# Delta rule: three buffers for a head's chain, the state load inside the chunk stage, and gate columns made in front as pairs

## The chip, the cores and the metric

The kernel runs on one core of a Trainium2 chip. The core has TensorE (PE in the profile, with its weight loads as PEld), VectorE (DVE), ScalarE (ACT), GpSimd (POOL) and SyncE (SP). Each engine takes its instructions in order. Here SP issues nearly all transfers between the main memory and the core's memory. The metric is device microseconds for one execution. Before the change three runs took 2188.87, 2191.32 and 2192.17 us: a median of 2191.32.

## What is computed

One layer of an encoder, for 512 prompt tokens and 8 x 16 sample tokens, 640 rows together, all in fp32:

```python
z = x @ w_in                                   # 2048 -> 12312 columns
q_a, k_a, v_a, f_a, gate_a, qkv_b, a_b, beta_b, gate_b, m_a, m_b = jnp.split(z, SPLIT_IDX, axis=-1)
# branch A: attention with forget gates, 8 heads of 128
y_a = (o_a * jax.nn.silu(gate_a)) @ w_out_fox
# branch B: delta rule, 8 heads of 128 x 128
conv = jax.nn.silu(sum(xpad[:, i:i + n_tok] * gdn_conv_w[i] for i in range(CONV_W)))
q_b, k_b, v_b = jnp.split(conv, [GDN_KEY_WIDTH, 2 * GDN_KEY_WIDTH], axis=-1)
o_b, s_new = gated_delta_chunked(q_b, k_b, v_b, g, beta, s0)
o_b = rms_norm(o_b, gdn_norm_w)
y_b = (o_b * jax.nn.silu(gate_b)) @ w_out_gdn
h = (jax.nn.sigmoid(m_a) * y_a + jax.nn.sigmoid(m_b) * y_b) @ w_out
x1 = layer_norm(DEEPNORM_ALPHA * x + h, ln_g, ln_b)
x_out = x1 + jax.nn.sigmoid(x1 @ w_pl_gate) * e    # e: rms_norm(p @ w_pl_proj)
```

`gated_delta_chunked` takes each chunk of tokens, solves a unit lower triangular system built from keys, decays and betas, and carries a 128 x 128 state from chunk to chunk. The sample rows start from stored states `s0`.

## The kernel before

**Columns.** The projections are made in columns of 128 output channels by 640 rows. A product in fp32 is made of three products of halves (high times high, high times low, low times high) in a fast fp32 form. In `column` (with `mm6`, L380 and L381) each of the 16 slices of the inner dimension needs 6 matmuls of 128x320. In `pair` (L458) two columns are made together, by a scheme with 7 products of half size instead of 8: 7 forms of 8 slices of 3 matmuls. A pair needs sums of weights, which VectorE makes (`w_sum`, L316) or, for some later columns, GpSimd in advance (`weight_sums`, loads L288, sums L292, stores L298). Weights come in tiles of 128x1024 (`wr`, L266), and are split into high and low by ScalarE (`wh`, L326) and VectorE (`wl`, L327), up to five pieces of 512 ahead of TensorE.

**Stages.** `front` makes the first columns, the values, and then `PAIRS` = 19 pairs: four of the attention gate, two of values, eleven of the merge gates (`FRONT` = 22 columns), two of query and key for heads 3 and 6. `phase_fox` makes the remaining queries and keys, and runs the attention between them. `phase_gdn` makes, per head of the delta rule, a column each of q, v, k and gate (`gq`, `gv`, `gk`, `gg`), and after some heads a merge column (`FILL`, `mcol`). Then come four plain and four half pairs of columns of `w_out_fox`, and `tail`.

**What sets the order.** There is one program order per engine, written by the Python code as it runs. While a column is made, `tick` is called once per slice (in a pair, once per two slices, so always once per six large matmuls). Generators in several lanes stand beside it; a tick lets each lane go a step, if its last `yield n` is n ticks ago and a planner's clock says that its inputs are there. The planner knows matmuls and the three other engines, but not when transfers land. `until(cond)` lets ticks pass without a column.

**A head of the delta stage.** `conv_silu` makes q, k, v. `gdn` makes decays, norms, and `lt` and `qk` (L948). `gdn_blocks` stores the 32x32 diagonal blocks (`ld`, L967), loads them spread over 80 partitions (`lanes`, L970), solves them on GpSimd in 31 steps (L978, L980), stores the result (`xd`, L985) and loads it as `u0` (L988), then the state `st` of the sample rows (L992). After `yield 8` it hands over to `gdn_chunks`, which copies `u0` on GpSimd (L1007) and runs `gdn_pro` (transposes `u0` on VectorE, L1101, first product L1110, then the four chunks) beside `gdn_dec` (sample rows, first use of `st` at L1059). `gdn_out` norms the output, multiplies it with the gate loaded from memory and stores it. The buffers of a head (`kt`, `vr`, `lt`, `qk`, `gr`, `kq`) exist twice, so `gdn` waits until the chunks of head h-2 are done (`chdone`), and `gdn_blocks` until those of h-1 are.

The gate column of a head goes through `silu_evac` (L807 to L809) and to memory in the delta stage.

Of the kernel before, what the change touches and what calls it, by code (L numbers as in the profile page):

```python
# [52 lines left out]
class Kernel:  # L53
# [8 lines left out]
    FRONT = 32 - 3 - 7  # L62
    PAIR0, PAIRS = 6, 6 + FRONT // 2 + 2
    BETWEEN = 6,
    APART = 3, 6
    FILL = 1, 1, 1, 0, 0, 0, 0, 4
# [430 lines left out]
    def consts2(self):  # L497
# [5 lines left out]
        self.nw = self.cv[:, 96:97]  # L503
# [297 lines left out]
    def silu_evac(self, ps, dst, tag):  # L801

        nc = self.nc
        for hf in range(2):
            sl = slice(hf * HALF, (hf + 1) * HALF)
            th = self.zt([P, HALF], tag, 1, "sc")
            nc.scalar.activation(th, ps[hf], AF.Tanh, scale=0.5)  # L807
            nc.vector.tensor_single_scalar(dst[:, sl], ps[hf], 0.5, op=ALU.mult)
            nc.vector.scalar_tensor_tensor(out=dst[:, sl], in0=th, scalar=1.0, in1=dst[:, sl], op0=ALU.add, op1=ALU.mult)  # L809


    def scale_e(self, re):

        nc = self.nc
        tags, e = [("kt", 2), ("vr", 2), ("lt", 2), ("qk", 2)], {}
# [30 lines left out]
    def conv_silu(self, strip, ct, h, c, dst):  # L846
# [18 lines left out]
        while self.done[c] < h - 2 + c % 2:  # L865
            yield
# [10 lines left out]
    def gdn(self, h, kq, v):  # L877
        nc, cb = self.nc, self.cb
        while not self.scaled or self.chdone < h - 2 or min(self.ready) < h:
            yield  # L880
        gr = self.zt([P, T], "gr", 2)
# [3 lines left out]
        kt = self.zt([P, 5, P], "kt", 2)  # L885
        vr = self.zt([P, 5, P], "vr", 2)
# [40 lines left out]
        cs = self.zt([P, 5, 5], "cs", 3)  # L927
# [12 lines left out]

        lt = self.zt([P, 5, P], "lt", 2)
        qk = self.zt([P, 5, P], "qk", 2)
# [19 lines left out]
    def gdn_blocks(self, h, kq, lt, qk, qg, kt, vr, cs):  # L962
# [24 lines left out]
        u0 = self.zt([P, 5, 32], "u0")  # L987
        nc.sync.dma_start(out=u0, in_=bass.AP(self.xd.tensor, self.xd.offset, [[32, P], [4096, 5], [1, 32]]))  # L988
        while self.chdone < h - 1:
            yield 2  # L990
        st = self.zt([P, 8, P], "st")
        nc.sync.dma_start(out=st, in_=self.i["st"][h])  # L992
        yield 8
        self.bdone = h
        self.chunks["gens"].append(self.gdn_chunks(h, kq, lt, qk, qg, kt, vr, cs, u0, st))

    def gdn_chunks(self, h, kq, lt, qk, qg, kt, vr, cs, u0, st):

        nc, uu = self.nc, self.uu
# [51 lines left out]
    def gdn_dec(self, h, qk, kt, vr, cs, st):  # L1051
# [3 lines left out]
        yield 6  # L1055
# [41 lines left out]
    def gdn_pro(self, h, kq, lt, qk, qg, kt, vr, cs, u0):  # L1097
# [4 lines left out]
        t1 = self.t1  # L1102
# [31 lines left out]
        x2 = self.zt([P, 4, 64], "sx2", 1, "x2")  # L1134
        nc.scalar.copy(out=x2[64:128].rearrange("p a b -> p (a b)"), in_=px[64:128, 0:256])
        yield 2
        px = self.sps()
        for t in range(4):
            nc.tensor.matmul(px[0:64, t * 64:(t + 1) * 64], x2[64:128, t, :], uu[64:128, t, 64:128],
                             start=True, stop=True)  # L1140
# [43 lines left out]
    def run(self, ctx):  # L1184
# [16 lines left out]
        self.sgd = [dr([P, T], F32, name=f"sgd{i}") for i in range(H)]  # L1201
        self.sgf = [dr([P, T], F32, name=f"sgf{i}") for i in range(H)]
# [43 lines left out]
    def front(self, work):  # L1246
# [122 lines left out]
        def vals(x, hf, z, u=None):  # L1369
# [7 lines left out]
            def close(h=2 * (n - 4) + 4 + x):  # L1377
# [28 lines left out]
        def heads(x, hf, z, u=None):  # L1406
# [8 lines left out]

            def close(h=self.APART[n - 6 - self.FRONT // 2]):
                if x == 0:
                    nc.scalar.mul(o, o, FOX_SCALE)
                nc.sync.dma_start(out=self.qkd[h, x], in_=m[x])
                if x:  # L1420
                    nc.sync.dma_start(out=self.o["fk"][h], in_=m[x])
# [4 lines left out]
        def weights():  # L1426
# [3 lines left out]
            yield from self.weight_sums([t[:, x:x + 256] for t in ws for x in (0, 256)], slice(0, 10), (6, 4, 2))  # L1430
        self.sums["gens"].append(weights())
        for n in range(self.PAIRS):
# [21 lines left out]
            self.pair(xf, gates if n < 4 else vals if n < 6 else merges if n < 6 + self.FRONT // 2 else heads, back)  # L1454
            if n < 4:
                self.ng += 2
            elif 6 <= n < 6 + self.FRONT // 2:
                self.nm += 2
# [4 lines left out]
    def phase_fox(self, work):  # L1463
# [14 lines left out]
        self.sums["gens"].append(self.weight_sums([ws[:, x:x + 256] for x in range(0, 1024, 256)], slice(10, 12),  # L1478
# [56 lines left out]
    def phase_gdn(self, conv, work):  # L1535
# [6 lines left out]
        self.sums["gens"].append(self.weight_sums([ws[:, x:x + 171] for x in range(0, 684, 171)], slice(12, None),  # L1542
                                                  (8, 6, 4)))
        self.uu = self.zt([P, 5, P], "uu")
        self.t1 = self.zt([64, 4, 64], "t1")
        self.kpad = self.zt([P, 8, 32], "kpad")
        self.gpad = self.zt([P, 8, 32], "gpad")
        for x in (self.uu, self.t1, self.kpad, self.gpad):
            nc.gpsimd.memset(x, 0.0)

        self.kqs = [self.zt([P, 2, T], f"kq{i}") for i in range(2)]
# [3 lines left out]
        self.scaled, self.chdone, self.bdone = False, -1, -1  # L1555
        self.ends["gens"].append(self.scale_e(re))
        self.untapped = 0
        for h in range(H):
            for c in range(4):
                acc = self.column()[0]  # L1560
                kq = self.kqs[h % 2]
                if c == 1:
                    v = self.zt([P, T], "v")
                if c == 3:
                    sg = self.zt([P, T], "sg")
                    self.silu_evac(acc, sg, "gth")
                    nc.sync.dma_start(out=self.sgd[h], in_=sg)
                else:
                    self.until(lambda: self.untapped == 0)
                    ct = 8 * (0, 2, 1)[c] + h  # L1570
                    self.untapped += 1
                    stp = self.strip_evac(acc, ct)
                    conv["gens"].append(self.conv_silu(stp, ct, h, c,
                                                       v if c == 1 else kq[:, 1 - c // 2, :]))
# [10 lines left out]
        def load(k, tag, to=raw):  # L1585
            to[k] = self.zt([P, {"ws": 684, "lanes": 1024}.get(tag, T)], tag, 2 if tag in ("kt", "vr", "lt", "qk", "gr") else 1,
# [742 lines left out]
def _layout(a):  # L2329
# [18 lines left out]
    for b in [*bg, *_wblock(seg["v"])[4:], *m[:nf], *[x[h] for h in Kernel.APART for x in (bq, bk)]]:  # L2348
# [10 lines left out]
    for h in range(H):  # L2359
        bl += [gq[h], gv[h], gk[h], gg[h]]  # L2360
# [80 lines left out]
```

## Time and profile before

| | |
|---|---|
| median of three runs | 2191.32 us |
| the profiled execution | 2187.32 us, of it 2185.5 us span |
| TensorE busy | 2165.9 us (99%) |
| VectorE, ScalarE, GpSimd busy | 67%, 43%, 26% |
| mean granted TensorE clock | 0.999 |
| front with its pairs | up to about 573 us |
| delta stage, from its first GpSimd work | from about 878 us |
| last use of a solved head, L1110 | 1586 us |

Matmuls overlap in the engine: a row's mean duration is that of one matmul from start to end, and is longer than the distance to the next. Counts in a stretch are those of the records; a plain fp32 product leaves two records. A row of waits says who ended an engine's idle time, not who caused the lateness.

### The profile page before, as it was taken

The page shows a single profiled execution, that of the slowest core. Times are in us where ns is not written, and L with a number is a line of the kernel's source. Part 1 is how long each engine was busy: PE and PEld are TensorE (multiplying, and loading weights), DVE is VectorE, ACT ScalarE, POOL GpSimd, SP SyncE. Part 2 cuts the span into 40 slices and gives each one's busy share as a digit, 9 for nine tenths or more (in the row PEclk, how much of TensorE's full clock was granted, in tenths as well). Part 3 has the DMA queues.
Part 4 walks back from the last instruction along what each step waited for, and adds up shares of the span by engine and source line. Part 5 has one row for each costly group of instructions (what it writes and reads, how often), then busy time and mean ns, then how long its engine had stood idle before and what let it go on. Part 6 is the DMA issues. An engine that isn't in the chain of part 4 may idle for free. (4 is left out here: it accounts for less than half of the span.)

```text
span 2185.5 us, 41824 instructions
## 1 busy us (share of the span) xinstructions
PE 2165.9 (99%) x15582; PEld 2099.0 (96%) x15582; DVE 1458.6 (67%) x2705; ACT 931.3 (43%) x2065; POOL 578.1 (26%) x1046
## 2 busy tenths in 40 slices
PE   9999999999999999999999999999999999999998
PEld 7799999999999999999999999999999999999998
DVE  5877677667545546755556566565657787789987
ACT  4344444444333335344345345345443343354544
POOL 0023223333011110216817637556600000011100
PEclk9999999999999999999999999999999999999999
DMA  6356665666687876854454444446566656674465
GB/s 233 104 184 197 198 189 185 196 193 204 236 317 256 309 267 199 290 167 126 121 156 131 130 126 142 123 131 196 167 243 245 221 167 205 195 274 133 149 229 171
DMA packets 222284, 421.12 MB, mean 193 GB/s; under 512 B 33768, under 2 KB 118840, under 8 KB 222080
## 3 DMA queue, kind: packets, MB, share of 16 engines
q1 hardware_dynamic: 222080, 418.45, 58.7%
q8 instruction: 122, 2.00, 0.4%
q14 instruction: 82, 0.67, 0.1%
HBM read 323.29 MB, written 95.07 MB: 191 GB/s over the span
## 5 line engine op out<-in xcount | busy, mean ns | idle before, releaser
L327 DVE TENSOR_TENSOR wl<-wr,wh 128x512 fp32r<-128x512 f32 x636 | 450.2, 717 | 349.0 <-ACT wh L326 340.1
L326 ACT CAST wh<-wr 128x512 fp32r<-128x512 f32 x636 | 388.5, 618 | 316.8 <-PE g L381 136.2
L380 PE MATMUL g<-xh,wh 128*128 128x320 f32 (+1 forms) x1152 | 375.9, 326 | 0.0
L380 PE MATMUL g<-xl,wh 128*128 128x320 f32 (+1 forms) x1152 | 356.1, 309 | 0.6 <-DVE xl L355 0.6
L381 PE MATMUL g<-xh,wh 128*128 128x320 f32 x1152 | 356.3, 309 | 0.0
L381 PE MATMUL g<-xl,wh 128*128 128x320 f32 x1152 | 355.9, 309 | 0.0
L380 PE MATMUL g<-xh,wl 128*128 128x320 f32 (+1 forms) x1152 | 355.8, 309 | 0.0
L381 PE MATMUL g<-xh,wl 128*128 128x320 f32 x1152 | 355.6, 309 | 0.0
L458 PE MATMUL g<-xh,wh 128*128 128x320 f32 (+1 forms) x1104 | 343.9, 311 | 2.7 <-ACT m L1240 1.6
L458 PE MATMUL g<-xl,wh 128*128 128x320 f32 (+1 forms) x1104 | 341.9, 310 | 0.6 <-DVE xl L355 0.6
L458 PE MATMUL g<-xh,wl 128*128 128x320 f32 (+1 forms) x1104 | 342.0, 310 | 0.0
L292 POOL TENSOR_TENSOR ws<-ws 128x171 f32<-128x171 f32 (+2 forms) x184 | 137.7, 748 | 658.0 <-DMA ws<-in_w 650.1
L380 PEld LDWEIGHTS g<-xh,wh 128*128 128x128 f32 x1152 | 217.0, 188 | 12.4 <-issue 8.6
L458 PE MATMUL g<-t,wh 128*128 128x320 f32 (+1 forms) x992 | 220.2, 310 | 0.0
L381 PEld LDWEIGHTS g<-xh,wh 128*128 128x128 f32 x1152 | 217.2, 189 | 1.0
L380 PEld LDWEIGHTS g<-xl,wh 128*128 128x128 f32 x1152 | 216.9, 188 | 1.1 <-DVE xl L355 1.1
L381 PEld LDWEIGHTS g<-xl,wh 128*128 128x128 f32 x1152 | 216.6, 188 | 0.0
L380 PEld LDWEIGHTS g<-xh,wl 128*128 128x128 f32 x1152 | 216.4, 188 | 0.2
L381 PEld LDWEIGHTS g<-xh,wl 128*128 128x128 f32 x1152 | 216.4, 188 | 0.0
L458 PEld LDWEIGHTS g<-xh,wh 128*128 128x128 f32 x1104 | 207.9, 188 | 4.5 <-ACT m L1240 2.1
L458 PEld LDWEIGHTS g<-xl,wh 128*128 128x128 f32 x1104 | 207.6, 188 | 1.1 <-DVE xl L355 1.1
L458 PEld LDWEIGHTS g<-xh,wl 128*128 128x128 f32 x1104 | 208.0, 188 | 0.0
(443 smaller groups left out, 3774.1 us busy)
## 6 DMA issues: line engine op xcount, KB each, us to landing
wr<-in_w SPq DMA_DIRECT2D x258, 512.0 KB
kc<-in_kc SPq DMA_DIRECT2D x32, 512.0 KB
vc<-in_vc SPq DMA_DIRECT2D x32, 512.0 KB
ws<-in_w SPq DMA_DIRECT2D x96, 128.0 KB
md<-m SPq DMA_DIRECT2D x32, 320.0 KB
t<-md SPq DMA_DIRECT2D x32, 320.0 KB
sr<-in_w SPq DMA_DIRECT2D x19, 512.0 KB
ws<-in_w SPq DMA_DIRECT2D x100, 85.5 KB
```

The costliest lines, as they stand in the source:

```text
L292: nc.gpsimd.tensor_tensor(out=o, in0=x, in1=y, op=op)
L326: nc.scalar.copy(out=hi, in_=src)
L327: nc.vector.tensor_tensor(out=lo, in0=src, in1=hi.bitcast(F32), op=ALU.subtract)
L380: nc.tensor.matmul(ps[0], whl[w], xhl[o][:, a], start=(first and x == 0), stop=(last and x == 2))
L381: nc.tensor.matmul(ps[1], whl[w], xhl[o][:, b], start=(first and x == 0), stop=(last and x == 2))
L458: nc.tensor.matmul(ps, a[:, w], b, start=(k == 0 and n == 0 and not more), stop=(k == last and n == 2), skip_group_check=True)
```

## The change

Eight more columns, the delta rule's gates, are made in the front as four pairs (`NG` = 8 gate columns and 8 more, stored in `sgf`, of which `sgd` is now the second half). One pair of merge columns leaves the front (`FRONT` = 20) and its two columns join the delta stage as fillers after heads 3 and 4. `PAIRS` becomes 22. A factor 0.5 of the gate moves into the norm weight `nw`. The GpSimd weight sums are dealt out as 12, 2 and 3 to the three stages; it was 10, 2 and 5.

In the delta stage `kt`, `vr`, `qk`, `gr` and the keys get three buffers. `lt` keeps two and is guarded by a new mark, `merged`, set once the chunk stage has read it. `gdn` may start when the chunks of head h-3 are done, and `gdn_blocks` loads `u0` (two buffers now) when those of h-2 are. The state is loaded by `gdn_chunks` itself. `x2` shares the tile of `t1`. Last, the scratch for software-made transfers is 1024 bytes.

```diff
-    FRONT = 32 - 3 - 7
-    PAIR0, PAIRS = 6, 6 + FRONT // 2 + 2
+    FRONT = 32 - 5 - 7
+    NG = 8
+    PAIR0, PAIRS = 6, NG + 2 + FRONT // 2 + 2
-    FILL = 1, 1, 1, 0, 0, 0, 0, 4
+    FILL = 1, 1, 1, 1, 1, 0, 0, 4
...
-        while self.done[c] < h - 2 + c % 2:
+        while self.done[c] < h - (2, 1, 3)[c]:
             yield
...
-        while not self.scaled or self.chdone < h - 2 or min(self.ready) < h:
+        while not self.scaled or self.chdone < h - 3 or min(self.ready) < h:
             yield
-        gr = self.zt([P, T], "gr", 2)
+        gr = self.zt([P, T], "gr", 3)
...
+        while self.merged < h - 2:
+            yield
         lt = self.zt([P, 5, P], "lt", 2)
-        qk = self.zt([P, 5, P], "qk", 2)
+        qk = self.zt([P, 5, P], "qk", 3)
...
         nc.sync.dma_start(out=self.xd, in_=x.rearrange("p c i -> p (c i)"))
         yield 5
-        u0 = self.zt([P, 5, 32], "u0")
+        while self.chdone < h - 2:
+            yield 2
+        u0 = self.zt([P, 5, 32], "u0", 2)
         nc.sync.dma_start(out=u0, in_=bass.AP(self.xd.tensor, self.xd.offset, [[32, P], [4096, 5], [1, 32]]))
-        while self.chdone < h - 1:
-            yield 2
+        yield 4
+        self.chunks["gens"].append(self.gdn_chunks(h, kq, lt, qk, qg, kt, vr, cs, u0))
+
+    def gdn_chunks(self, h, kq, lt, qk, qg, kt, vr, cs, u0):
+
+        nc, uu = self.nc, self.uu
         st = self.zt([P, 8, P], "st")
         nc.sync.dma_start(out=st, in_=self.i["st"][h])
-        yield 8
-        self.bdone = h
-        self.chunks["gens"].append(self.gdn_chunks(h, kq, lt, qk, qg, kt, vr, cs, u0, st))
...
         self.ob = ob = self.zt([P, 5, P], "ob")
-        yield 6
+        yield 9
...
-            yield from self.weight_sums([t[:, x:x + 256] for t in ws for x in (0, 256)], slice(0, 10), (6, 4, 2))
+            yield from self.weight_sums([t[:, x:x + 256] for t in ws for x in (0, 256)], slice(0, 12), (6, 4, 2))
...
-            for c in range(4):
+            for c in range(3):
                 acc = self.column()[0]
-                kq = self.kqs[h % 2]
+                kq = kqs[:, h % 3:4 + h % 2:3 + h % 2 - h % 3]
                 if c == 1:
                     v = self.zt([P, T], "v")
-                if c == 3:
-                    sg = self.zt([P, T], "sg")
-                    self.silu_evac(acc, sg, "gth")
-                    nc.sync.dma_start(out=self.sgd[h], in_=sg)
...
-    nc = _bacc.Bacc("TRN2", target_bir_lowering=False, num_devices=1)
+    nc = _bacc.Bacc("TRN2", target_bir_lowering=False, num_devices=1, dynamic_dma_scratch_size=1024)
```

The diff shows little of how instructions move. Two places on SP do. The first is the last head's chain, head 7. Before (`out_stp` is the end of head 6's chunks, `xd` the solve's store of head 7, `og` a gate load, `fd` and `wr` belong to the columns):

```order
L1180 DMA out_stp<-S 128x128
L1017 DMA og<-sgd_174 128x640
L985 DMA xd<-sx 80x256
L266 DMA wr<-ws102b 128x1024
L1680 DMA fd_18360<-fx 128x640
L988 DMA u_19082<-xd 128x5x32
L992 DMA st<-in_st 128x1024
L1680 DMA fd_18361<-fx 128x640
```

The same place in the changed program:

```order
L978 DMA xd<-sx 80x256
L267 DMA wr<-in_w 128x1024
L1667 DMA fd_18356<-fx 128x640
L983 DMA u_18890<-xd 128x5x32
L1172 DMA out_stp<-S 128x128
L991 DMA st<-in_st 128x1024
L267 DMA wr<-ws102S_191 128x1024
L1009 DMA og<-sgf_182 128x640
```

The end of head 6's chunks now stands behind the solve's store and the `u0` load of head 7, and the state load follows it: before, head 6 was over when head 7's solve ended.

The second place is the border from `front` to `phase_fox`. Before (`xq` reloads parts of x, `qkd` and `out_fk` store the last pair, then `q` and `k` are the attention's first loads):

```order
L1449 DMA xq<-in_xT 128x320 x8
L266 DMA wr<-in_w 128x1024
L1419 DMA qkd_189<-m_1163 128x640
L1421 DMA out_fk<-m_1163 128x640
L1419 DMA qkd_188<-m_1162 128x640
L1492 DMA q<-qkd_184 128x640
L1492 DMA k<-qkd_185 128x640
```

In the changed program:

```order
L1441 DMA xq<-in_xT 128x320 x8
L267 DMA wr<-in_w 128x1024
L1411 DMA qkd_189<-m_1165 128x640
L1413 DMA out_fk<-m_1165 128x640
L1411 DMA qkd_188<-m_1164 128x640
L299 DMA ws128S_227<-ws 128x256
L299 DMA ws128b<-ws 128x256
L299 DMA ws128S_228<-sb 128x256
L299 DMA ws128S_230<-sb 128x256
L1485 DMA q<-qkd_184 128x640
L1485 DMA k<-qkd_185 128x640
```

Four stores of the last GpSimd weight sum now stand between the last pair's stores and the attention's first loads.

74 lines of the change are left out of this document (32 added, 42 removed).

## The prediction

> **What bounds the kernel now.** I read the page first, then busy time by stretch, then the waits of TensorE, then the timeline of the delta stage. The page:
>
> ```profile
> span 2185.5 us, 41824 instructions
> PE 2165.9 (99%) x15582; PEld 2099.0 (96%) x15582; DVE 1458.6 (67%) x2705; ACT 931.3 (43%) x2065; POOL 578.1 (26%) x1046
> PEclk9999999999999999999999999999999999999999
> ```
>
> TensorE is busy from end to end at full granted clock; no other engine passes 67%. Time can only come from fewer or cheaper matmuls, or from its few gaps. The next view is busy time in stretches of 100 us: one stretch in the front's pairs, two in the delta stage, and the end.
>
> ```profile
> core 0: us, PE busy (x) PEld busy (x) DVE busy (x) ACT busy (x) POOL busy (x), PEclk, DMA share, GB/s
> 300.00:400.00 100.00, 100.00 (x683) 100.00 (x682) 70.98 (x94) 40.40 (x76) 31.13 (x30) 1.00 0.59 187
> 1200.00:1300.00 100.00, 98.64 (x798) 93.45 (x797) 57.38 (x134) 42.62 (x121) 52.99 (x121) 1.00 0.43 130
> 1400.00:1500.00 100.00, 98.94 (x750) 95.85 (x749) 57.30 (x137) 48.78 (x153) 68.09 (x137) 1.00 0.41 130
> 2100.00:2186.00 86.00, 78.03 (x526) 77.76 (x524) 68.82 (x121) 36.96 (x60) 0.00 (x0) 0.97 0.56 187
> ```
>
> In the front nothing but large matmuls runs: 683 in 100 us, so one large matmul costs **0.1464 us**, while the page's durations of about 309 ns overlap. In the delta stage TensorE idles about 1 us in 100; only the last 86 us have a real hole (8 us), and nothing there changes. Who makes TensorE wait:
>
> ```profile
> engine line waited for: us in total, times, longest us
> PE s L1110 <- DVE m L1101: 2.7, 3, 1.4
> ```
>
> The longest entry, 2.7 us, is the first product of a head's chunk waiting for the transpose of its solved blocks. The change works at exactly that place.
>
> **The matmuls.** A plain column is 16 slices of 6 matmuls, 96; a pair of columns is 7 forms of 8 slices of 3, 168 instead of 192. Before there are 6 + 22/2 + 2 = 19 front pairs, after 8 + 2 + 20/2 + 2 = 22. Eight gate columns leave the delta stage and two merge columns join it (FILL sums to 9, it was 7): six plain columns fewer. So +3 x 168 - 6 x 96 = **-72 matmuls**, and 72 x 0.1464 = **-10.5 us**. The front grows by 3 x 168 x 0.1464 = 73.8 us, the delta stage loses 84.3 us.
>
> The row gives 146.4 ns for 320 columns. The Trainium skill, "TensorE: Matmul & The Clock Gate", section "Back-to-back issue gap", gives N/2.4 + 2.5 ns for isolated matmuls, 135.8 ns for N = 320, and says that the weight loads set the spacing too; by that formula the saving would be 9.8 us, an estimate. The trace has the larger spacing, and PEld is as busy as PE beside it.
>
> **Work that moves without a price.** The gate's evacuation leaves the delta stage and a tanh and a multiply of 640 columns per gate join the front:
>
> ```profile
> L809 DVE SCALAR_TENSOR_TENSOR sg<-sc,sg 128x320 f32<-128x320 f32 x16 | 9.3, 581 | 0.5
> L808 DVE TENSOR_SCALAR sg<-g 128x320 f32<-128x320 f32 x16 | 7.8, 490 | 12.4 <-ACT sc L807 12.4
> L1362 DVE SCALAR_TENSOR_TENSOR m<-sa,m 128x640 f32<-128x640 f32 x8 | 6.6, 821 | 3.5 <-ACT sa L1361 3.5
> L316 DVE TENSOR_TENSOR sr<-wr,sr 128x1024 f32<-128x1024 f32 x38 | 50.0, 1316 | 0.0
> L292 POOL TENSOR_TENSOR ws<-ws 128x171 f32<-128x171 f32 x100 | 65.5, 655 | 71.5 <-DMA ws<-in_w 66.5
> L292 POOL TENSOR_TENSOR ws<-ws 128x169 f32<-128x169 f32 x20 | 12.5, 626 | 17.6 <-DMA ws<-in_w 16.5
> ```
>
> 17.1 us of VectorE leaves the delta stage and 6.6 us joins the front; each new pair also needs its weight sums, two of 1.3 us and two much like them. VectorE has 29 us idle in each 100 there while TensorE is full, so this costs nothing as long as casts stay ahead; without that cover the three pairs' sums, some 16 us, would show. GpSimd makes five weight sums in the delta stage (65.5 + 12.5 us, 15.6 each); three remain, and 31 us leave it. The fox stage keeps two, and the front, where GpSimd is 31% busy, makes two more. The halved norm weight is one tiny extra operation. The smaller scratch only frees memory: all but 204 of 222284 DMA packets are on the hardware queue, and their issuing rows are SP's.
>
> **Front to fox.** At the front's end SP now has the last weight sum's stores ahead of the fox stage's first loads, and the first ScalarE casts of that stage stand in line behind those loads. Times before, at that border:
>
> ```profile
> 573.46 0.31 PE L380 MATMUL g<-xh,wh 128*128 128x320 f32 x1
> 575.97 0.32 SPq L1419 DMA_DIRECT2D qkd<-m  x1
> 578.25 0.32 SPq L1492 DMA_DIRECT2D q<-qkd  x1
> 575.85 0.60 ACT L326 CAST wh<-wr 128x512 fp32r<-128x512 f32 x1
> 581.62 0.51 ACT L657 CAST qh<-q 128x384 fp32r<-128x384 f32 x1 [5.16 <-DMA q<-qkd]
> 584.46 1.29 DVE L327 TENSOR_TENSOR wl<-wr,wh 128x512 fp32r<-128x512 f32 x2
> ```
>
> The load of q waits 2.3 us for the last store to land. ScalarE stands 5.16 us; the next weight piece is ready at 584.46 + 1.29/2, about 585.1. Five pieces of 24 matmuls (3.5 us each) are ahead, so TensorE needs the sixth at 573.46 + 17.6 = 591.1: 6 us to spare. Four more stores at the row's 0.32 us each add 1.3 us, and if the last lands as late as this one, q is 1 to 4 us later: inside the 6. Price 0; if 4 became 10, it would be 4 us.
>
> **The head's chain.** Per head: the blocks go to memory (L967), GpSimd solves them, the result is stored (L985), u0 is loaded (L988), transposed (L1101), and TensorE's L1110 uses it. Heads 1, 4, 5, 7 and the one row of head 6:
>
> ```profile
> 1100.80 0.43 SPq L988 DMA_DIRECT2D u<-xd  x1
> 1108.13 0.44 PE L1110 MATMUL s<-m,lt 32*32 32x32 f32 x16
> 1354.11 0.38 SPq L988 DMA_DIRECT2D u<-xd  x1
> 1366.93 0.44 PE L1110 MATMUL s<-m,lt 32*32 32x32 f32 x16
> 1374.99 1.77 SPq L967 DMA_DIRECT2D ld<-lt  x4
> 1435.43 0.34 SPq L985 DMA_DIRECT2D xd<-sx  x1
> 1437.09 0.38 SPq L988 DMA_DIRECT2D u<-xd  x1
> 1443.34 0.44 PE L1110 MATMUL s<-m,lt 32*32 32x32 f32 x16 [1.06 <-DVE m L1101]
> 1458.52 1.98 SPq L967 DMA_DIRECT2D ld<-lt  x4
> 1528.31 1.77 SPq L967 DMA_DIRECT2D ld<-lt  x4
> 1580.03 0.33 SPq L985 DMA_DIRECT2D xd<-sx  x1
> 1581.75 0.37 SPq L988 DMA_DIRECT2D u<-xd  x1
> 1585.84 0.31 DVE L1101 STREAM_TRANSPOSE m<-u 128x128 f32<-128x128 f32 x1 [2.25 <-DMA u<-xd]
> 1586.20 0.44 PE L1110 MATMUL s<-m,lt 32*32 32x32 f32 x16
> ```
>
> From load to use the last head took 4.45 us, the shortest and with the transpose already waiting; heads 1, 4, 5 took 7.3, 12.8, 6.25, so they have 2.9, 8.4 and 1.8 us in hand. The program now spaces the start by 4 ticks after the u0 load instead of 8. A tick is six large matmuls, 0.88 us, so 3.5 us go. That alone would give 0.6, 0, 1.7 and 3.5 us of wait, for eight heads twice that, 11.6 us.
>
> The other way to see it is by the period. Last head: store of blocks to solve's end 51.7 us (1528.31 to 1580.03), to first use 57.9 us. Head 5, with weight sums in GpSimd's queue, took 60.4 us to the solve's end. What TensorE has to do meanwhile: from 1458.52 to 1528.31 are 69.8 us with four columns, 4 x 96 x 0.1464 = 56.2, which leaves 13.6 us of the chain's own products. With three columns it is 42.2 + 13.6 = 55.8 us. Heads 0 to 4 still get a fourth column (a merge); heads 5 to 7 have three, and stand **2.1 us** short of 57.9 even with no weight sum near. The blocks go one head at a time, and 51.7 + 1.7 to the u0 load fits into 55.8, so the lack does not pile up. Three heads at 2.1 are 6.3 us, less the 2.7 already waited: **+3.6 us**. Lower end: -2.7, all present waits gone, since 31 us of weight sums leave this queue and a third buffer lets a head's products begin earlier. Upper end: each of the three like head 5, 60.4 + 6.2 (1580.03 to 1586.20) = 66.6, or 10.8 short, 32.4 - 2.7 = +29.7. I take +3.6, nearest the last head's row, because the sums should be over by then:
>
> ```profile
> 883.23 2.32 POOL L292 TENSOR_TENSOR ws<-ws 128x171 f32<-128x171 f32 x4 [3.54 <-DMA ws<-in_w]
> 1522.57 1.11 POOL L292 TENSOR_TENSOR ws<-ws 128x169 f32<-128x169 f32 x2
> 1582.17 0.73 SPq L992 DMA_DIRECT2D st<-in_st  x1
> 1588.53 0.64 PE L1059 MATMUL s<-st,kpad 128*32 128x128 f32 x16
> ```
>
> Five sums take 640 us, 128 each, so three end some 384 us into the stage. Head 5's blocks leave 1375.0 - 883.2 = 492 us in now, and 56 us earlier after the change (six gate columns fewer, two merge columns more): 436. The state, loaded just behind u0 now and at the chunk's start after the change, costs nothing: its first use (L1059) stands nine ticks, 7.9 us, behind the load, and the last head used it 6.4 us after issue without waiting.
>
> Sum: -10.5 + 3.6 = **-6.9 us**. The profiled execution took 2187.3 us (span 2185.5 and 1.8 around it): 2180.4. The median shown lies 4 us above it, so I write 2191.3 - 6.9 = **2184 us**.
>
> **Rivals.**
> 1. *All of it arrives*, and the chain's waits vanish in the third buffer: 10.5 to 13.2 us, 2179 us. For it: the waits now are 2.7 us in eight heads. Against: 55.8 below 57.9. Chance 0.25.
> 2. *The waits eat the gain*: heads 5 to 7, and one or two more, wait 3 to 4 us each, some 11 us: 2190 us. For it: heads 1, 5 and 7 have at most 2.9 us in hand and lose 3.5. Chance 0.18.
> 3. *Slower: GpSimd's solve sets the pace.* Place: L1110 of heads 5 to 7 (and with it SP, which stands at the solve's store with weight loads behind it). Price 10.8 us a head, net +19.2: 2210 us. It beats the saving once a head needs (10.5 + 2.7)/3 = 4.4 us more than 55.8, so from 60.2 us on. For it: head 5's 60.4 us to the solve's end alone. Against: fewer weight sums there. Chance 0.11.
> 4. *The border front to fox* starves TensorE because q comes over 6 us later: about 4 us lost, 2188 us. Chance 0.06.
>
> On rival 3: by the Trainium skill, "TensorE: Matmul & The Clock Gate", Part 1, a pause of about 3.4 us lets the clock fall to half until a further 3.4 us of work; by that each such wait would cost 1.7 us more, an estimate. The rows show 1.00 through the stage and 0.97 only in the last stretch, where TensorE does pause.
>
> **How the numbers follow.** The forecast has 0.40. What a measurement of this kernel can tell from no change is about 0.2%, 4.4 us. Faster: rival 1 whole (0.25), the forecast but for its upper tail (0.34), parts of 2 and 4 (0.06): 0.65. Slower: rival 3 and a tail of 2: 0.13. The rest 0.22. The range 2175 to 2196 holds the forecast (2180 to 2188 by itself), rivals 1, 2 and 4, and leaves out rival 3 and runs below the lower end.
>
> **What would show it.** Large matmuls 72 fewer at 0.146 us; the front's end near 573.5 + 73.8 = 647 us; PE 99%; a line of waits at the first product of the chunk (L1102 after the change) between 3 and 10 us; no ScalarE wait over 11 us for q. Wrong if that line exceeds 15 us, or if PE idles at the border, or if the front's pairs run slower than 683 in 100 us with three more of them.

## The result, and the profile after

The changed kernel takes 2214.38 us (median of four runs, 2210.96 to 2218.18) beside 2191.15 us for the kernel before on the same chip: a ratio of 1.0108, 95% interval 1.0085 to 1.0131. It is 23 us slower, where 2184 us were forecast. The profiled executions are 2187.32 and 2211.32 us, 24.0 apart. First the page of the changed kernel:

```profile
span 2209.5 us, 41696 instructions
PE 2166.9 (98%) x15510; PEld 2097.0 (95%) x15510; DVE 1489.1 (67%) x2726; ACT 944.3 (43%) x2086; POOL 572.6 (26%) x1031
PEclk9999999999999999999999999999999999999999
```

The 72 matmuls are gone (15582 to 15510 records). Yet TensorE is busy 1.0 us *longer*, and its idle time, span less busy time, went from 19.6 to 42.6 us. By the forecast's own count it should be busy 2165.9 - 10.5 = 2155.4 us. So the 24 us are -10.5 for the matmuls, +23.0 of idle time, and +11.5 of matmuls that ran slower (+1.0 measured, -10.5 expected). Busy time by stretch says where; first after, then one row of before (columns: stretch, its length, TensorE's busy time and records, granted clock, DMA share, GB/s):

```profile
0.00:640.00 640.00, 635.67 (x4189) 1.00 0.59 190
640.00:700.00 60.00, 54.80 (x418) 0.97 0.85 288
700.00:1000.00 300.00, 299.86 (x2465) 1.00 0.80 269
1000.00:1660.00 660.00, 636.53 (x4797) 0.99 0.45 140
```

```profile
1000.00:1660.00 660.00, 655.26 (x4989) 1.00 0.48 151
```

5.2 us are lost between 640 and 700 us, where the front goes over to the softmax stage, and 23.5 us in the delta stage, where 4.7 were lost before. The waits of TensorE in the changed kernel (in total, times, longest):

```profile
PE s L1102 <- DVE m L1093: 9.9, 2, 6.4
PE s L880 <- DVE kqs L858: 7.2, 3, 5.1
PE s L748 <- ACT qh L659: 3.8, 1, 3.8
PE s L1079 <- POOL vm L1063: 1.8, 1, 1.8
```

L1102 is the first product of a head's chunk, which was L1110; L880 are the transposes of a head's q, k and v; L748 the first scores of the softmax stage. The last head, from the timelines of all engines (the first line is the store of its blocks):

```profile
1522.12 1.91 SPq L960 DMA_DIRECT2D ld<-lt  x4
...
1527.52 3.96 SPq L1575 DMA_DIRECT2D ogr<-ogd  x5
1531.53 0.77 SPq L963 DMA_DIRECT2D lanes<-ld  x1
1538.48 0.93 POOL L971 TENSOR_TENSOR sx<-eye,lanes 80x248 f32<-80x248 f32 x1 [14.60 <-DMA lanes<-ld]
1578.68 0.33 SPq L978 DMA_DIRECT2D xd<-sx  x1
1580.80 0.37 SPq L983 DMA_DIRECT2D u<-xd  x1
1585.09 0.31 DVE L1093 STREAM_TRANSPOSE m<-u 128x128 f32<-128x128 f32 x1 [9.34 <-DMA u<-xd]
1585.45 0.64 PE L1102 MATMUL s<-m,lt 32*32 32x32 f32 x16 [6.41 <-DVE m L1093]
```

VectorE stands 9.34 us with the transpose, and TensorE behind it 6.41. The chain from store to first product is 63.3 us; TensorE arrived after 56.9. The solve itself is 40.1 us (1538.48 to the copies behind it at 1578.59), but its input was asked for only 9.4 us after the store: eight other transfers stand between on SP, most of them loads for work to come. Before, with the store at 1528.31 and five transfers between, it was 6.5 us, and the solve began 5.7 us after that, not 6.9:

```profile
1534.81 0.78 SPq L970 DMA_DIRECT2D lanes<-ld  x1
1540.47 0.72 POOL L978 TENSOR_TENSOR sx<-eye,lanes 80x248 f32<-80x248 f32 x1 [8.16 <-DMA lanes<-ld]
```

The second way in which the solve is late does not pass through u at all. The strip of a column, which the convolution reads, gets 24 elements by a small copy on GpSimd (L834). When the plan puts that copy behind the steps of a solve, ScalarE (L845), VectorE (L848) and then TensorE wait in turn:

```profile
1304.64 0.85 ACT L845 ACTIVATE cy<-strip,taps 128x664 f32<-128x664 f32 x1 [5.02 <-POOL strip L834]
1305.52 1.12 DVE L848 SCALAR_TENSOR_TENSOR cy<-strip,taps,cy 128x664 f32<-128x664 f32 x1 [5.10 <-ACT cy L845]
1313.69 0.64 PE L1102 MATMUL s<-m,lt 32*32 32x32 f32 x16 [3.49 <-DVE m L1093]
...
1465.61 0.65 DVE L858 SCALAR_TENSOR_TENSOR kqs<-cth,cy 128x512 f32<-128x512 f32 x1
1466.32 1.12 PE L880 MATMUL s<-cb,kqs 128*128 128x128 f32 x4 [5.14 <-DVE kqs L858]
```

At head 3 VectorE starts 5.10 us late and its backlog makes the transpose late; before the 5.14 us the same happens by 3.63 and 3.01 us at 1456. The sum of these waits is no measure of the loss: ScalarE waited as long in the kernel before (first line), where no gap of TensorE in the delta stage was longer than 1.4 us. What is new is where they fall.

```profile
ACT cy L854 <- POOL strip L843: 18.1, 8, 3.4
ACT cy L845 <- POOL strip L834: 17.4, 6, 5.0
```

The border, from SP, ScalarE and TensorE:

```profile
651.53 0.32 SPq L1411 DMA_DIRECT2D qkd<-m  x1
651.94 0.38 SPq L299 DMA_DIRECT2D ws128S<-ws  x1
652.42 0.42 SPq L299 DMA_DIRECT2D ws128b<-ws  x1
652.96 1.74 SPq L299 DMA_DIRECT2D ws128S<-sb  x2
656.88 0.32 SPq L1485 DMA_DIRECT2D q<-qkd  x1
660.04 0.51 ACT L659 CAST qh<-q 128x384 fp32r<-128x384 f32 x1 [8.02 <-DMA nbd<-sfd]
660.88 0.46 PE L748 MATMUL s<-k,q 128*128 128x128 f32 x2 [3.76 <-ACT qh L659]
```

From the last store of the head rows to q's load are 5.35 us; it was 2.28 before, and TensorE did not wait. Last, the clock in stretches of 2 us behind the longest gap:

```profile
1584.00:1586.00 2.00, 0.55 (x16) 0.50 1.05 384
1586.00:1588.00 2.00, 2.00 (x11) 0.50 0.72 272
1588.00:1590.00 2.00, 2.00 (x9) 0.50 0.23 93
1590.00:1592.00 2.00, 2.00 (x35) 0.97 0.27 104
```

The granted clock falls to 0.50 behind each of the four gaps of 3.5 us and more (3.76 at the border, then 3.49, 5.14 and 6.41) and stays there for 3 to 5 us. Half of the time that TensorE is busy at 0.50 is 1.6, 1.7, 2.2 and 2.3 us behind these four, together about 8 us of the 11.5; what makes up the rest is not shown (e13 below has no such dip and is still busy 4.0 us longer than the 2155.4). Behind the gap of 1.82 us (L1079, at 1549) the clock stays at 1.00. The Trainium skill, "TensorE: Matmul & The Clock Gate", Part 1, gives half clock after an idle window of about 3.4 us; the five gaps of this trace agree with it, but shorter gaps in other runs, shown in the last section, do not, and there the measurement decides.

### The profile page after: what moved, and what is told of

It reads as the page before. It is cut to its first block, busy times and chain, and to the rows that moved or that the text cites. A ratio compares the mean times of both kernels' runs of the same rounds, so it can differ in the third digit from the quotient of the medians.

```text
span 2209.5 us, 41696 instructions
## 1 busy us (share of the span) xinstructions
PE 2166.9 (98%) x15510; PEld 2097.0 (95%) x15510; DVE 1489.1 (67%) x2726; ACT 944.3 (43%) x2086; POOL 572.6 (26%) x1031
## 3 DMA queue, kind: packets, MB, share of 16 engines
q1 hardware_dynamic: 217472, 418.45, 57.9%
## 5 line engine op out<-in xcount | busy, mean ns | idle before, releaser
L382 PE MATMUL g<-xh,wh 128*128 128x320 f32 x1056 | 328.0, 311 | 0.0
L382 PE MATMUL g<-xl,wh 128*128 128x320 f32 x1056 | 327.2, 310 | 0.0
L382 PE MATMUL g<-xh,wl 128*128 128x320 f32 x1056 | 326.7, 309 | 0.0
L293 POOL TENSOR_TENSOR ws<-ws 128x256 f32<-128x256 f32 (+2 forms) x144 | 113.0, 785 | 678.7 <-DMA ws<-in_w 673.1
L459 PE MATMUL g<-t,wh 128*128 128x320 f32 (+1 forms) x1040 | 230.5, 310 | 2.6 <-DVE t L468 1.3
L459 PEld LDWEIGHTS g<-xh,wh 128*128 128x128 f32 x1200 | 225.9, 188 | 3.4 <-ACT m L1232 2.1
L459 PEld LDWEIGHTS g<-xl,wh 128*128 128x128 f32 x1200 | 225.6, 188 | 1.1 <-DVE xl L356 1.1
L459 PEld LDWEIGHTS g<-xh,wl 128*128 128x128 f32 x1200 | 226.0, 188 | 0.4 <-DVE wl L328 0.4
L381 PEld LDWEIGHTS g<-xh,wh 128*128 128x128 f32 x1056 | 200.1, 189 | 14.4 <-issue 9.3
L382 PEld LDWEIGHTS g<-xh,wh 128*128 128x128 f32 x1056 | 200.5, 190 | 1.0
L381 PEld LDWEIGHTS g<-xl,wh 128*128 128x128 f32 x1056 | 200.0, 189 | 0.8 <-DVE xl L356 0.8
L382 PEld LDWEIGHTS g<-xl,wh 128*128 128x128 f32 x1056 | 199.8, 189 | 0.0
L381 PEld LDWEIGHTS g<-xh,wl 128*128 128x128 f32 x1056 | 199.4, 189 | 0.1
L382 PEld LDWEIGHTS g<-xh,wl 128*128 128x128 f32 x1056 | 199.1, 189 | 0.0
```

The source lines that it names most:

```text
L293: nc.gpsimd.tensor_tensor(out=o, in0=x, in1=y, op=op)
L381: nc.tensor.matmul(ps[0], whl[w], xhl[o][:, a], start=(first and x == 0), stop=(last and x == 2))
L382: nc.tensor.matmul(ps[1], whl[w], xhl[o][:, b], start=(first and x == 0), stop=(last and x == 2))
L459: nc.tensor.matmul(ps, a[:, w], b, start=(k == 0 and n == 0 and not more), stop=(k == last and n == 2), skip_group_check=True)
```

## The experiments

The first theory: GpSimd's solve, which the plan takes to be shorter than it is, comes too late in a stage with fewer columns, both at the first product and by way of the strip. Rivals: only the shortened distance of 4 ticks is at fault (A); the loss is the clock by itself (B); the buffers or the moved state load are (C). Each change below is against the changed kernel unless said otherwise, and each ratio is to the kernel before, with its 95% interval.

### e1: a shorter solve in the same order

```diff
-            nc.gpsimd.tensor_tensor(out=tmp[:, :, 0:n], in0=xo[:, :, j:j + 1].to_broadcast([80, 8, n]), ...
+            nc.gpsimd.tensor_tensor(out=tmp[:, 0:1, 0:n], in0=xo[:, 0:1, j:j + 1].to_broadcast([80, 1, n]), ...
```

The subtraction likewise; the planner is told the old sizes. One of eight columns is solved and the other seven are filled by one more copy per head, so this kernel's results are not those of the layer. But for that, every engine's written order is the changed kernel's.

> GpSimd's triangular solve computes one of its eight columns, the other seven are copies of the unit matrix (the delta rule's numbers are therefore not the reference's); the order of all instructions on all engines stays. Theory (the solve, planned shorter than it runs, is late in a stage with fewer columns, and reaches TensorE both directly and through the small strip copies behind it): the solve falls by about 62 x 0.17 = 10.5 us a head, the 9.9 us of waits at the first small product (L1102) and the 7.2 us at the transposes (L880) fall to under 4 together, TensorE's idle time from 42.6 to about 27, and the time to 2190 to 2198. Rival A (the loss is at the front-to-fox border or spread over the stage): 2209 to 2216. Rival B (the loss is the lower clock by itself): idle time falls but the time stays over 2205.

2188.91 us, ratio 0.9996 (0.9987 to 1.0005). GpSimd is busy 463.4 instead of 572.6 us, 13.7 less a head. TensorE's two longest waits in e1, where L753 and L885 are the first scores and the transposes:

```profile
PE s L753 <- DMA k<-qkd: 4.0, 1, 4.0
PE s L885 <- DVE kqs L863: 2.1, 2, 1.1
```

The waits at the first product are gone from the list, the 7.2 us at the transposes became 2.1, and ScalarE never waits for a strip; TensorE's idle time is 25.4 us. With every instruction in its old place, a shorter solve brings back 25 us: in this order, the solve is what is late. Rivals B and C do not explain this run; A, a start too near to the load of u, would give the same here. VectorE is also busy 30 us less in e1 (1459.1 for 1489.1); that this is not what pays is argued from e16, which is faster with 1498.8, and no run separates it. The border (4.0 us) stays.

### e2, e8: the distance behind the load of u

```diff
-        yield 4
+        yield 8        # e2; yield 6 in e8
         self.chunks["gens"].append(self.gdn_chunks(h, kq, lt, qk, qg, kt, vr, cs, u0))
```

> The chunk stage follows the load of u by 8 planner ticks, as in the kernel before, instead of 4 (yield 8 for yield 4); all else as in the changed kernel. Rival A (only this shortened distance is at fault): the wait at L1102 goes and with it the clock's dips, 2190 to 2197. Theory (the solve is late against the columns, and what it delays also passes through the strip copies): the direct wait at head 7 shrinks by up to 3.5 us of 6.4, the waits at L880 by way of the strip stay, 2203 to 2211.

2187.85 us, ratio 0.9990 (0.9980 to 0.9999), much better than the theory allowed. Nearly all of the delta stage's loss is back (653.38 us busy of the 660 from 1000 to 1660), and ScalarE's waits for strips fell from 17.4 to 6.0 us. TensorE's two longest waits in e2:

```profile
PE s L748 <- DMA k<-qkd: 3.8, 1, 3.8
PE s L1051 <- DMA st<-in_st: 1.8, 1, 1.8
```

What is left is the border, and a wait for the state that the changed kernel did not have. So rival A explains the size of the loss as well as the theory does.

> 6 ticks instead of 4 (8 gave 2187.9). If the distance acts smoothly: 2196 to 2206, the wait at L1102 near 5 us. If 8 ticks helped by an order of the plan that merely happens to be better: no such step, 2186 to 2190 or 2210 to 2220.

2207.25 us, ratio 1.0074 (1.0059 to 1.0090): between the two, but above the range expected of a smooth effect, and the waits at L1102 are 2.6 us, not 5. The longest are now at the border (4.6) and the transposes (3.1). Three points do not show that the effect is smooth, as e16 will tell.

### e3, e4, e6: the change's parts apart

e3 takes the buffers, the state load and the distance back to what they were before and keeps the gate pairs in front. e4 is the kernel before with three buffers, the state load inside the chunk stage and 4 ticks; e6 is e4 with 8. All three have the smaller scratch.

> Gate columns made in front as pairs, and the smaller DMA scratch; the delta stage keeps two buffers, the state load ahead of the chunk stage and the 8 ticks. Theory (fewer columns per head leave the solve without cover, whatever the buffers): as slow as the changed kernel or slower, 2208 to 2225, with waits at L1102 or L880 of over 12 us in the trace. Rival C (the three buffers and the moved state load are at fault, the pairs give their 10.5 us): 2178 to 2184.

> Three buffers, state load inside the chunk stage, 4 ticks and the smaller DMA scratch; the gate columns stay four to a head in the delta stage, as before. Theory (four columns cover the solve): within 5 us of the kernel before, 2186 to 2196. Rival C (the buffers and the moved load are at fault): 2200 to 2215.

> Three buffers and the state load inside the chunk stage with four columns to a head (as in e4), but 8 ticks after the load of u. If the shortened distance is what made e4 slower: 2187 to 2193, the waits at the first small product (7.4 us in e4) gone. If the buffers or the moved state load are: 2201 to 2207; of it the 6.0 us that TensorE waited for the state should stay in either case unless the 4 more ticks do not matter to it.

e3: 2231.57 us, ratio 1.0185 (1.0169 to 1.0200). e4: 2204.94 us, 1.0066 (1.0051 to 1.0081). e6: 2185.05 us, 0.9977 (0.9968 to 0.9987). TensorE's two longest waits in e4, at the first product and the first use of the state:

```profile
PE s L1111 <- DVE m L1102: 7.4, 4, 2.8
PE s L1060 <- DMA st<-in_st: 6.0, 2, 4.2
```

Both are gone in e6, whose delta stage is full but for 1.0 us (658.99 busy of the 660 from 1000 to 1660). So with four columns to a head the 4 ticks cost 19.9 us: a lack of columns is not needed for the loss, against the theory. Here the wait for the state goes with the ticks; but e2 has 8 ticks and a wait of 1.8 us for it, and the changed kernel 4 ticks and none, so the distance alone does not decide it. The pairs with two buffers and the old place of the state load (e3) are the slowest of these: TensorE is idle 49.2 us there, at a mean clock of 0.987. With the buffers and the moved load, at the same 8 ticks, they take 2187.9 us (e2), so these two, with the new order that comes with them, are worth 43.7 us once the columns are gone: rival C falls.

### e7, e10: the strip's copies off GpSimd

```diff
-        nc.gpsimd.memset(st[:, 0:3], 0.0)
+        nc.vector.memset(st[:, 0:3], 0.0)
...
-        nc.gpsimd.tensor_copy(out=sv[:, :, 0:3], in_=self.cvst[:, ct, :].rearrange("p (b r) -> p b r", r=3))
+        nc.scalar.copy(out=sv[:, :, 0:3], in_=self.cvst[:, ct, :].rearrange("p (b r) -> p b r", r=3))
```

Here, and in e5, e9, e10, e12 and e14 to e18, two waits in the planner keep head h's output (`ob`, one buffer) from being written before head h-1's is read; they stand ahead of L1066 in `gdn_dec` and ahead of the chunk loop in `gdn_pro`:

```diff
+        while self.gdone < h - 1:
+            yield 1
```

> The changed kernel (4 ticks) with the small strip copies on ScalarE and their clearing on VectorE instead of GpSimd, and the two planner waits of e5. Theory (part of the lateness reaches TensorE through the strip copies that stand behind the solve on GpSimd): ScalarE's 17.4 us of waits for the strip go, and with them the gaps of 3.5 us (head 3) and 5.1 us (head 7's transposes); the direct wait for u at head 7 (6.4 us) stays: 2198 to 2206. If the strip is only a symptom: 2210 to 2216.

> As e9 with the sums as in the changed kernel (12, 2, 3). Compared with e2 (2187.9) only the strip's copies leave GpSimd: 2183 to 2188, ScalarE's 6.0 us of waits for the strip gone; the 3.8 us at the border (L748) and its dip of the clock stay. e9 should be 4 to 7 us faster than this one.

e7: 2196.84 us, ratio 1.0030 (1.0020 to 1.0040). ScalarE's 17.4 us of waits for GpSimd's strip copies are gone (4.1 us of waits for VectorE's clearing have come), and the long wait at the transposes with them (1.5 us are left of 7.2). TensorE's two longest waits in e7, at the first product and the first scores:

```profile
PE s L1104 <- DVE m L1095: 6.8, 3, 4.3
PE s L748 <- DMA k<-qkd: 5.3, 1, 5.3
```

e10, with 8 ticks: 2190.37 us, 1.0002 (0.9992 to 1.0011), no better than e2 and above the 2183 to 2188 expected. The figure of e7 is just below the theory's 2198 to 2206, but the two planner waits change the order too (e16), so the 17.5 us below the changed kernel cannot be put to the strip alone.

### e5, e9, e12, e13: the twelfth weight sum at the border

Counts of GpSimd's weight sums in front, softmax and delta stage: 12, 2, 3 in the changed kernel. All four kernels have 8 ticks. e5 has 11, 2, 4; e12 has 11, 3, 3; e9 is e12 with the strip off GpSimd. e13 keeps 12, 2, 3 and makes the front's sums 11 ticks apart instead of 12, so that the last one ends earlier:

```diff
-            yield from self.weight_sums([...], slice(0, 12), (6, 4, 2))
+            yield from self.weight_sums([...], slice(0, 12), (5, 4, 2))
```

> 8 ticks after the load of u, and 11 weight sums in the front instead of 12 (2 in the softmax stage, the others in the delta stage); two waits in the planner keep head 7's output from being written before head 6's is read. If the twelfth sum is what delays q and k at the border: the 3.8 us wait at head 0's first scores (L748) and the clock's dip behind it go, 5 us less than with 8 ticks alone, 2181 to 2185. If q and k are late for another reason: 2186 to 2190, with the wait still there.

> As e9 with the strip's copies on GpSimd. If e5 was slower than e2 because its delta stage had a fourth sum on GpSimd: 2180 to 2185, with no wait over 1 us at L748 and the waits at the transposes (L880) back under 2 us. If it was the loss of the border wait that moved everything else: 2192 to 2197 as in e5.

> 8 ticks after the load of u, the strip's small copies on ScalarE and VectorE, and the weight sums 11 in front, 3 in the softmax stage, 3 in the delta stage (so the delta stage has no sum more than the changed kernel, unlike e5); the two planner waits of e5. If border, strip and distance are what ate the 10.5 us of the pairs and nothing else is: TensorE busy 2155 to 2158, idle 20 to 23, 2176 to 2181, faster than both kernels. If the third sum disturbs the softmax stage or something else stays: 2184 to 2190.

> 8 ticks after the load of u, and the twelve sums of the front made 11 ticks apart instead of 12 (waits 5, 4, 2 for 6, 4, 2), so that the twelfth ends before the head rows are stored: on SyncE the four stores ahead of q's load are gone from there, on GpSimd nothing changes its order. If those stores and the sum itself are what delays q and k: the wait at L748 (3.8 us in e2) and the clock's dip are gone, 5 to 6 us less than e2's 2187.9, 2181 to 2184. If the weight loads of the border are late for themselves: 2186 to 2190, the wait moves to L327 or L381.

e5: 2194.42 us, 1.0020 (1.0010 to 1.0029), slower than both readings had it. The border wait is gone, but ScalarE again waits 16.6 us for strips in the delta stage, and TensorE 5.7 us at transposes. e12: 2215.55 us, 1.0123 (1.0108 to 1.0138), and e9: 2219.21 us, 1.0133 (1.0117 to 1.0150). My expectation for these two was wrong, for a reason that I had not thought of; TensorE's longest wait in e12, and what ScalarE waits for there:

```profile
PE g L381 <- ACT e L1745: 21.2, 1, 21.2
946.89 0.42 ACT L1745 COPY e<-g 128x320 f32<-128x320 f32 x1 [22.40 <-DMA ws138S<-ws]
```

The third sum does not end with its stage: a column is evacuated (L1745) into buffers that the sum still uses, and TensorE stands 21.2 us. e13: 2184.82 us, 0.9978 (0.9968 to 0.9987). The wait at L748 has left the list. In the stretch from 640 to 700 us the profile of e2, and then that of e13, shows:

```profile
640.00:700.00 60.00, 55.31 (x418) 0.94 0.85 286
```

```profile
640.00:700.00 60.00, 58.47 (x462) 1.00 0.81 272
```

3.2 us of idle time are gone, and about 2.5 us of lowered clock (half of the 5.0 us that TensorE was busy at 0.50). The written order of VectorE, ScalarE and GpSimd is the same in both kernels; TensorE's differs in 12 rows at the border, and SP's in the transfers of the sums. So this is the border's price nearly by itself: 5.7 us in this stretch, 6.0 between the profiled executions, but 3.0 between the medians, where the intervals of the two ratios overlap.

### e11, e14, e15: the planned length of the solve, and more distance

```diff
-        a, b = ((0.17, 0.0011), (0.21, 0.00085), (0.25, 0.0020))[e]
+        a, b = ((0.17, 0.0011), (0.21, 0.00085), (0.30, 0.0028))[e]      # e11, e15: GpSimd's cost in the planner
```

> The changed kernel (4 ticks) with the planner's cost of a GpSimd instruction raised from 0.25 + 0.0020 per element to 0.30 + 0.0028, nearer to the 0.95 us that the profile shows for 248 elements: the plan itself now places the solve's end, the load of u and the chunk stage later. Theory (the solve is planned shorter than it runs): the waits at L1102 fall below 3 us and the time to 2188 to 2200. If the plan's cost is not the cause: 2208 to 2220.

> As e13 with 10 ticks after the load of u. If the head's chain still lacks distance at 8 ticks (e2 had 1.8 us of waits for the state and 1.7 us at the transposes): 2 to 4 us below e13, 2177 to 2182. If 8 ticks are enough: within 2 us of e13, or slower by the later ends of the heads, 2182 to 2188.

> As e13 with the planner's GpSimd cost of e11 (0.30 + 0.0028 per element). If the plan's cost and the distance answer the same lateness: no gain over e13, 2180 to 2187. If they add up: 2175 to 2180.

e11 (4 ticks): 2194.84 us, 1.0030 (1.0018 to 1.0041). The waits at L1102 are gone, 20 us are back, and a new wait of 5.8 us for an output (L1028) appears. e14 (10 ticks): 2188.20 us, 0.9986 (0.9978 to 0.9995); e15 (8 ticks, e11's cost and e13's sums): 2200.59 us, 1.0042 (1.0030 to 1.0054). Its idle time lies between 1600 and 1700 us (15.5 us, 7.8 in e11), where waits of 5.8 us at an output and 5.0 us at a first product stand. e15 is slower than both readings had it. A longer planned solve helps where the distance is short; on top of 8 ticks it brings nothing. How much of e14's and e15's loss against e13 comes with the two planner waits, which e13 does not have, is open.

### e16: the changed kernel with 4 ticks, without the border's wait

The sums as in e13, the two planner waits of e7, nothing else.

> The changed kernel (4 ticks) with the front's twelve sums 11 ticks apart (and the two planner waits of e5). If border and distance are separate losses: 3 to 6 us below the changed kernel's 2214, 2208 to 2211, the wait at L748 gone, the waits of the delta stage as they were. If the border's loss only moves: 2212 to 2217.

2182.17 us, ratio 0.9964 (0.9950 to 0.9977): the lowest median of all (e17's interval overlaps), 32 us below the changed one, and with 4 ticks. I had expected 3 to 6 us. First some of TensorE's waits in e16 (L1160 is a product of the chunk loop, L1104 the first product), then its busy time in the delta stage:

```profile
PE s L1160 <- ACT vn L1157: 2.7, 1, 2.7
PE s L880 <- DVE kqs L858: 1.7, 2, 0.9
PE s L1104 <- DVE m L1095: 0.9, 1, 0.9
```

```profile
1000.00:1660.00 660.00, 654.12 (x4974) 1.00 0.47 148
```

TensorE is busy 2156.5 us, 9.4 less than before the change, and idle 22.0. So neither 4 ticks nor three columns make a head late of themselves, and rival A falls as the whole cause. The sums' spacing alone moves only the 12 rows at the border. The rest comes with the two planner waits: compared with the written order of the changed kernel they move some 400 rows of TensorE in more than 100 places, and rows of the four other engines with them. They were not run without the border's edit, but by subtraction of the border's 3 to 6 us, 26 to 29 us stand to them. Counted in the written order, as sixes of large matmuls (one tick each) between the last product of L941 and the first of L1102:

| kernel | heads 0 to 7 | us |
|---|---|---|
| before | 70 68 68 62 66 64 64 62 | 2191 |
| e4, four columns, 4 ticks | 66 64 66 62 60 60 58 56 | 2205 |
| e6, four columns, 8 ticks | 70 66 68 60 64 64 65 59 | 2185 |
| changed, and e1 | 64 62 60 60 56 60 59 68 | 2214, 2189 |
| e8, 6 ticks | 64 62 60 62 58 61 71 77 | 2207 |
| e2 and e13, 8 ticks | 66 70 72 62 68 60 67 73 | 2188, 2185 |
| e16 | 64 62 56 60 62 58 66 75 | 2182 |
| e17 | 66 70 68 62 62 70 57 59 | 2183 |
| e3, two buffers, 8 ticks | 66 72 64 65 37 36 52 60 | 2232 |
| e15, 8 ticks, longer planned solve | 84 104 114 112 110 103 99 79 | 2201 |

In the changed kernel's order heads 4 and 6 stand nearer to their blocks than in e2 by 12 and 8, and the last head by 5; e16 gives these three 6 or 7 more without another tick. e3, with 37 and 36, is the slowest kernel of the table. But this number alone does not decide: e17 has 57 and 59 at its last heads and takes 2183 us, e8 has 71 and 77 and takes 2207, and e15, with the most of all, takes 2201.

### e17, e18: the heads with three columns

```diff
-    FILL = 1, 1, 1, 1, 1, 0, 0, 4
+    FILL = 1, 1, 1, 1, 0, 1, 1, 3      # e17; 1, 1, 1, 0, 1, 1, 0, 4 in e18
```

Both are e13 otherwise, with the two planner waits.

> e13 with the merge columns at heads 0, 1, 2, 3, 5, 6 and three after head 7 (FILL 1, 1, 1, 1, 0, 1, 1, 3 for 1, 1, 1, 1, 1, 0, 0, 4). If the heads with three columns are still short at 8 ticks (my prediction's count by columns): the waits of e13 between 1500 and 1600 us (2.9 us idle) go, 2179 to 2183. If the distance is all that counts: 2183 to 2188.

> e13 with the three-column heads apart (FILL 1, 1, 1, 0, 1, 1, 0, 4: heads 3, 6 and 7 instead of 5, 6 and 7). By the count of columns: head 3's first product waits 2 us more, head 5's less, 2182 to 2187. If the distance is all that counts: within 2 us of e13's 2184.8.

e17: 2183.16 us, 0.9969 (0.9958 to 0.9979), at the edge of what both readings expected, its interval overlapping e13's, with 1.2 us idle between 1500 and 1600 us for e13's 2.9; e18: 2191.91 us, 1.0008 (0.9998 to 1.0018), worse than both. Its longest waits, 4.8 and 3.0 us, stand at later products of the chunks (L1155, L1133), not at a first product. The count of columns to a head forecasts neither.

## Why the prediction was wrong, point by point

**What bounds the kernel.** Right: TensorE is full, and each wait that is added shows in the time.

**The matmuls, -10.5 us.** Right. 72 records fewer; the first scores of the softmax stage moved from 584.0 to 660.9 us, of which 3.8 is the wait, so the front grew by 73.1 (73.8 forecast). Where no long wait stands in the way (e16) the busy time is 9.4 us less and the median 9.0.

**Work without a price.** Right for VectorE, whose casts make TensorE wait no longer than before. The weight sums that leave GpSimd were worth nothing to the last head: its solve took 40.1 us, and I had expected less lateness from a freer queue.

**Front to fox, price 0.** Wrong. ScalarE's cast came as late as I had bounded it (q's load 3.1 us later behind the store of the head rows, inside "1 to 4"), but the 6 us to spare were counted to the sixth weight piece. TensorE's own next instruction, the scores of head 0, needs q and k before that. It waited 3.76 us, with half clock behind it: 3.0 us between the medians of e2 and e13, 6.0 between their profiled executions. Rival 4 had this place and 4 us.

**The head's chain, +3.6 us.** This is the step that failed, by its size. The time that TensorE has per head was right where it can be compared: 55.8 us forecast, 56.9 at the last head. What the chain needs was taken from one row of before, 57.9 us, the last head's; head 5's rows, shown beside it, give 68.4 (1374.99 to 1443.34). After the change the last head's was 63.3, 5.4 us more: 2.9 because SP asked for the lanes 9.4 us after the blocks' store, not 6.5, 1.3 because they came later after that, and 1.2 in the solve and behind it. That is 6.4 late where 2.1 was forecast. "The lack does not pile up" was wrong in another way: the lateness left the solve by the strip copies, at heads where u was in time, and gave gaps of 3.49 and 5.14 us at places that the step does not have. And I had two readings, "3.5 us less distance" at 11.6 us and the period at 3.6, and kept the smaller. In the delta stage 18.8 us of idle time were added (23.5 less 4.7), five times the term.

**The clock.** The prediction's sentence on the Trainium skill ("TensorE: Matmul & The Clock Gate", Part 1) estimated 1.7 us for each such wait; the four gaps cost 1.6 to 2.3 us each, about 8 together. It stood outside the sum, and the sum needed it.

**Rival 3** ended nearest, 2210 us for 2214, with the right culprit in the order that was built. That its figure came so near is luck, since its mechanism did not hold: the period of three-column heads is not what counts, since four columns lose 19.9 us in the same way (e4, e6) and three need not lose anything (e16).

**State load, price 0.** Right for the changed kernel; in e2 and e4 TensorE waited 1.8 and 6.0 us for it.

**The signs.** The front's end (647.3 us) and the line at L1102 (9.9 us, "between 3 and 10") came as forecast, and TensorE idled at the border, which was named as a sign of being wrong. No sign watched the transposes of q, k and v (7.2 us), where the strip copies showed.

**What stays open.** The changed kernel's loss is shown to be the late solve in its order (e1), and several small shifts of the plan remove it (e2, e11, e16). Which of the rearranged rows does it is not settled: more than 100 places move together, and neither ticks, nor columns, nor the distance in the table forecast all the runs.

## What to carry to other kernels

When a generator's delay is cut in a plan with in-order queues, do not cost the delay itself: the whole stage is dealt out anew, and 2 ticks or a planner's wait moved this kernel by 7 to 29 us. Compare, in the new written order, each long helper chain with the work that must cover it, though that distance alone did not forecast the time here, and follow the small instructions that stand behind that chain on its engine. And a border between stages is priced by the first instruction that needs the late transfer on the bound engine itself, not by the pieces in its queue. Add half clock, here 1.6 to 2.3 us each, to every gap of 3.5 us, and count a gap of 1.5 to 3 us as one that may have it too.

## What was not expected of the hardware

Behind gaps of 3.49 us and more the granted clock was 0.50 for 3 to 5 us, behind 1.82 us it stayed at 1.00; the profile's mean over the whole run, 0.994 against 0.999, hides this. But the length of a gap alone does not decide: in e2 the clock fell to 0.50 for about 3.4 us behind a gap of 1.77 us (from 1520.48), in e10 behind one of 1.50, while in e16 it stayed at 1.00 behind 2.74 (until 1446.64). First e2, then e16:

```profile
1524.00:1526.00 2.00, 2.00 (x9) 0.50 0.95 319
```

```profile
1447.00:1449.00 2.00, 2.00 (x17) 1.00 0.00 0
```

One further surprise was the solve's cost in instructions rather than elements: with one eighth of the elements (e1) the 480 instructions behind the first pair of each head took about 0.28 us each instead of 0.51, so their busy time fell by less than half (244.3 to 135.6 us).
